# Where the token columns are cut: 384, 352, 352 and 256, 288 in place of 368, 368, 352 and 272, 272

## The chip, the core and the metric

The kernel runs on one core of a Trainium2 chip, as one program. The metric is the device time of one execution in microseconds (us). Before the change the median of three runs is 1601.55 us, the lowest 1600.8 and the highest 1601.77.

## What is computed

One inference step of a two-layer decoder trunk in float32. 1024 tokens of a prompt and 64 tokens of eight samples (eight each) go through the same weights, so there are 1088 token columns. The first layer is a Mamba-2 layer (input projection, short convolution, a chunked scan over the state, a gate, output projection), the second a pooling layer. The parts that matter here are the projections:

```python
def ssd_branch(h, conv_prev, ssm_prev, w_in, ..., w_out):
    zxbcdt = h @ w_in
...
    return gated.astype(h.dtype) @ w_out, new_conv, new_ssm

def pool_branch(h, pool_prev, start_pos, w_in, w_group, ch_scale, w_out):
    uz = h @ w_in
...
    mixed = jnp.einsum('blgc,gcd->blgd', pooled, w_group.astype(jnp.float32)).reshape(b, L, POOL_WIDTH)
    mixed = mixed * ch_scale.astype(jnp.float32) * jax.nn.silu(z)
    return mixed.astype(h.dtype) @ w_out, up[:, -POOL_STATE:]
...
y = rmsnorm(x, final_norm_g).astype(x.dtype)
```

## The kernel before, in words

Activations lie transposed: features on the 128 partitions, the 1088 token columns along the free dimension (64 sample columns last). Every projection is made of TensorE matmuls with a 128x128 weight tile as the stationary operand and a stretch of token columns as the moving one, accumulated in one PSUM tile of up to 512 float32 columns. For precision each operand is split in a high and a low part of type float32r, and each product is three matmuls: high weight by high token, high by low, low by high. Each of the three loads its own weights.

The token columns are cut in two ways.

**Plain projections** (`mm1` and `mm3`, L190 to L192; `op_first`, L807 to L812) cut the 1088 columns by the table `CH` (L21) in three chunks, at 0, 368 and 736, of 368, 368 and 352 columns. A weight tile goes over the three chunks in turn, each in its own PSUM tile. This is how half of the first layer's input projection is done (24 of 48 weight tiles, 20 of them beside the scan), its output projection, the first two tile pairs of the second layer's input projection, and that layer's group products.

**Half products** are used where an algorithm of the Strassen kind replaces eight block products by seven: most of the second layer's input projection and the other half of the first layer's (`fast_pair`, with `product`, L1051 to L1053), and the second layer's output projection (`out_product` with `op_half`, L1269 to L1271). They work on half of the tokens, `HALF` = 544 columns, and cut that half into two quarters of `QUART` = 272 columns, c = 0 and c = 1. In `product` a quarter is four weight tiles by three matmuls, 12 matmuls into one PSUM tile, and then the other quarter with the same weights; in `op_half` it is 8 by 3. `put` and `add` in `fast_pair`, and `contribute` (L1254, L1256), then add the PSUM tiles into sums in SBUF on VectorE, quarter by quarter, and ScalarE copies the first product of each seven out (L1077 and its like).

The end of the program (`pool_layer`, from L1781) runs the last of the seven output products quarter by quarter, so that the final normalization of the quarters that are ready runs beside the last matmuls: a sum of squares over the partitions by a matmul with ones (`ms_log`, L302 and L304), a logarithm and exponentials on ScalarE (L305, L1750, L318), the scaling on VectorE (L1763) and GpSimd (L1761), and the store.

Between the float32r matmuls of the projections stand others in plain float32 (the scan's, transposes, sums of squares). The order on each engine is made by a scheduler from the order of the code and its own estimates of duration.

Of the kernel before, what the change touches and what calls it, by code (L numbers as in the profile page):

```python
# [10 lines left out]
AF = mybir.ActivationFunctionType  # L11
ALU = mybir.AluOpType
# [4 lines left out]
NP = 1024  # L17
NS = 64
TOK = NP + NS
HALF, QUART = TOK // 2, TOK // 4  # L20
CH = ((0, 368), (368, 368), (736, 352))  # L21
KD = 8
EPS = 1e-6
GROUPS = (1, 2, 3, 0)
# [75 lines left out]
class Build:  # L100
# [936 lines left out]
    def product(self, tags, x):  # L1037
        nc = self.nc
        if x not in self.X:
            self.X[x] = [(t[:, :HALF], t[:, HALF:]) for t in (self.T[int(x[1]), k] for k in range(4))]  # L1040
        nxt = next(self.wgen, None)
        if nxt:
            self.wahead.append(nxt)
        else:
            self.stream_split(self.wpos)
        hi, lo = self.wahead.pop(0)
        ps = [self.pp.tile([P, 512], F32, tag=t, bufs={"mm": 3, "tr": 2, "y": 2, "S": 1}[t], name=self.name("st")) for t in tags]
        for c in range(2):
            t = slice(QUART * c, QUART * c + QUART)
            for k, (xh, xl) in enumerate(self.X[x]):  # L1050
                nc.tensor.matmul(ps[c][:, :QUART], hi[:, k], xh[:, t], start=(k == 0), stop=False)  # L1051
                nc.tensor.matmul(ps[c][:, :QUART], hi[:, k], xl[:, t], start=False, stop=False)  # L1052
                nc.tensor.matmul(ps[c][:, :QUART], lo[:, k], xh[:, t], start=False, stop=(k == 3))  # L1053
        return [q[:, :QUART] for q in ps]

    def fast_pair(self, u, z, after):


        nc, product = self.nc, self.product

        def add(out, x, y):
            nc.vector.tensor_tensor(out=out, in0=x, in1=y, op=ALU.add)

        def put(dst, half, c, x, y):
            t, o, rv = dst
            o += HALF * half + QUART * c
            n = QUART - NS if rv is not None and half and c else QUART
            add(t[:, o:o + n], x[:, :n], y[:, :n])
            if n < QUART:
                add(rv, *(v[:, n:].rearrange("p (b i) -> p b i", i=8) for v in (x, y)))  # L1070

        cs = [slice(QUART * c, QUART * c + QUART) for c in range(2)]
# [173 lines left out]
    def contribute(self, m, d, c, ps):  # L1246

        nc, x = self.nc, self.x
        for z, half, sign in SENDS[m]:
            e, a = d + 4 * z, HALF * half + QUART * c  # L1250
            pn = min(a + QUART, NP) - a
            g = (self.gat[1] if sign > 0 else self.ngat)
            g = g[:, e, 8:9] if sign > 0 else g[:, e:e + 1]
            ins = nc.vector.scalar_tensor_tensor(out=x[e][:, a:a + pn], in0=ps[:, :pn], scalar=g, in1=x[e][:, a:a + pn], op0=ALU.mult, op1=ALU.add)  # L1254
            if pn < QUART:
                ins = nc.vector.scalar_tensor_tensor(out=self.sacc[:, e], in0=ps[:, pn:QUART], scalar=float(sign), in1=self.sacc[:, e], op0=ALU.mult, op1=ALU.add)  # L1256
        return ins

    def op_tile(self):
# [3 lines left out]

    def op_half(self, w, blk, ks, c, ps):
        nc, (hi, lo) = self.nc, w
        a = QUART * c
        for k in ks:
            xh, xl = blk[k][:, a:a + QUART], blk[k][:, HALF + a:HALF + a + QUART]
            nc.tensor.matmul(ps[:, :QUART], hi[:, k], xh, start=k == 0, stop=False)  # L1269
            nc.tensor.matmul(ps[:, :QUART], hi[:, k], xl, start=False, stop=False)  # L1270
            nc.tensor.matmul(ps[:, :QUART], lo[:, k], xh, start=False, stop=k == 7)  # L1271

    def out_product(self, m, steps, then=None):

# [397 lines left out]
    def pool_layer(self):  # L1672
        nc, io, sl = self.nc, self.io, self.slots
# [41 lines left out]
        x = self.x = [None] * 8  # L1715
# [18 lines left out]
        for d in range(8):  # L1734
            t = self.mt.tile([P, NS], F32, tag="gs", bufs=2, name=self.name("gs"))
# [37 lines left out]
        blk = self.blocks[7]  # L1773
# [2 lines left out]
            self.ow_fetch()  # L1776
            self.ow_split()
        ws = ws[24:]
        sq, sqs = [], sl.get("sq")
        for c in range(2):  # L1780
            a = QUART * c  # L1781
            for d in range(4):
                ps = self.op_tile()
                self.op_half(ws[d], blk, range(8), c, ps)
                ins = self.contribute(7, d, c, ps)
                if c == 0:
                    with self.tc.issue_after(ins.ins):
# [3 lines left out]
                    square(d, 0, QUART)  # L1791
                else:
                    t = sqs[:, QUART * d:QUART * d + QUART]
                    nc.scalar.activation(t, x[d][:, a:a + QUART], AF.Square)
# [115 lines left out]
```

## Time and profile before

| | before |
|---|---|
| time, median of 3 runs | 1601.55 us |
| span of the profiled execution, first to last instruction | 1599.4 us |
| what lies around the span, by the median | 2.15 us |
| instructions in the trace | 30692 |
| matmul records | 11946 |
| bytes moved by DMA | 275.58 MB |

The profiled execution's own time is known by its span alone. A matmul's row gives its start and its modelled duration; matmuls are pipelined, so that one starts while others are under way. What a matmul costs in a dense stream is therefore the interval from its start to the next one's start, and not the mean duration of its group. A plain float32 matmul has two records in the trace, a float32r matmul has one.

### The profile page before, as it was taken

To read this page: it belongs to the slowest core of one execution; us is meant where nothing else is said; L and a number is where in the kernel's file an instruction comes from. 1 tells how busy PE (TensorE), PEld (TensorE's weight loads), DVE (VectorE), ACT (ScalarE), POOL (GpSimd) and SP (SyncE) were. 2 spreads that over 40 slices of the span, in tenths; PEclk is the share of its full clock that TensorE was granted. 3 is DMA by queue.
4 is the path that set the end of the run, shared out by engine and by line. 5 is a ranking of instruction groups with operands and counts; after the bars stand their busy time and mean duration, and the time that the engine had idled before them with its cause. 6 is when DMAs were issued, how large, how long until landed. Compare 5 with 4: busy or idle time off the path is not lost. (4 is left out here: it accounts for less than half of the span.)

```text
span 1599.4 us, 30692 instructions
## 1 busy us (share of the span) xinstructions
PE 1578.8 (99%) x11946; PEld 1505.4 (94%) x11946; DVE 1293.5 (81%) x2152; ACT 791.4 (49%) x1512; POOL 514.6 (32%) x558
## 2 busy tenths in 40 slices
PE   9999999999999999999999999999999999999997
PEld 7899999998889889888899899999999999999997
DVE  6874879778788888888989867998889867667886
ACT  6663344456676766675455437533323333233364
POOL 0133556512231313131212232275666640000241
PEclk9999999999999999999999999999999999999999
DMA  9423232355555554768899632142333279565683
GB/s 353 166 100 110 69 112 83 110 178 158 188 170 173 161 187 148 240 224 303 289 317 312 221 135 74 60 142 103 114 114 104 102 246 373 142 176 178 165 171 119
DMA packets 122305, 275.58 MB, mean 172 GB/s; under 512 B 18192, under 2 KB 59312, under 8 KB 122160
## 3 DMA queue, kind: packets, MB, share of 16 engines
q1 hardware_dynamic: 118128, 260.90, 47.3%
q0 software_dynamic: 4032, 12.72, 4.7%
q8 instruction: 94, 1.54, 0.4%
q14 instruction: 51, 0.42, 0.1%
HBM read 201.12 MB, written 70.23 MB: 170 GB/s over the span
## 5 line engine op out<-in xcount | busy, mean ns | idle before, releaser
L1051 PE MATMUL st<-hh,w 128*128 128x272 f32 x832 | 240.2, 289 | 0.9 <-ACT w L182 0.9
L1053 PE MATMUL st<-hh,w 128*128 128x272 f32 x832 | 240.4, 289 | 0.4 <-DVE w L184 0.4
L1052 PE MATMUL st<-hl,w 128*128 128x272 f32 x832 | 240.0, 288 | 0.0
L1051 PE MATMUL st<-t,w 128*128 128x272 f32 x624 | 179.7, 288 | 0.0
L1053 PE MATMUL st<-t,w 128*128 128x272 f32 x624 | 179.5, 288 | 0.0
L1052 PE MATMUL st<-t,w 128*128 128x272 f32 x624 | 179.2, 287 | 0.0
L190 PE MATMUL mm<-hh,wh 128*128 128x368 f32 (+1 forms) x528 | 178.3, 338 | 0.0
L192 PE MATMUL mm<-hh,wl 128*128 128x368 f32 (+1 forms) x528 | 173.7, 329 | 0.0
L191 PE MATMUL mm<-hl,wh 128*128 128x368 f32 (+1 forms) x528 | 173.1, 328 | 0.0
L1051 PEld LDWEIGHTS st<-hh,w 128*128 128x128 f32 x832 | 156.8, 188 | 1.4 <-ACT w L182 1.4
L1053 PEld LDWEIGHTS st<-hh,w 128*128 128x128 f32 x832 | 156.5, 188 | 0.9 <-DVE w L184 0.9
L1052 PEld LDWEIGHTS st<-hl,w 128*128 128x128 f32 x832 | 156.7, 188 | 0.0
L182 ACT ACTIVATE w<-wr 128x512 fp32r<-128x512 f32 x104 | 65.1, 631 | 166.2 <-PE st L1053 137.3
L623 POOL TENSOR_TENSOR hd<-h,cd 128x256 f32<-128x256 f32 x56 | 45.9, 820 | 301.0 <-DVE h L624 144.9
L1270 PE MATMUL op<-b,w 128*128 128x272 f32 x448 | 128.9, 288 | 0.8 <-DVE b L1199 0.7
L1269 PE MATMUL op<-b,w 128*128 128x272 f32 x448 | 129.5, 289 | 0.0
L1271 PE MATMUL op<-b,w 128*128 128x272 f32 x448 | 128.9, 288 | 0.0
L190 PE MATMUL mm<-gh,wh 128*128 128x368 f32 (+1 forms) x372 | 125.5, 338 | 0.0
L192 PE MATMUL mm<-gh,wl 128*128 128x368 f32 (+1 forms) x372 | 122.4, 329 | 0.0
L191 PE MATMUL mm<-gl,wh 128*128 128x368 f32 (+1 forms) x372 | 122.0, 328 | 0.2 <-DVE gl L783 0.2
L1051 PEld LDWEIGHTS st<-t,w 128*128 128x128 f32 x624 | 117.7, 189 | 0.1
L1053 PEld LDWEIGHTS st<-t,w 128*128 128x128 f32 x624 | 117.3, 188 | 0.0
(307 smaller groups left out, 4576.5 us busy)
## 6 DMA issues: line engine op xcount, KB each, us to landing
wr<-win SPq DMA_DIRECT2D x48, 512.0 KB, 4.2
acb<-acd SPq DMA_DIRECT2D x64, 256.0 KB, 4.4
wr<-pin SPq DMA_DIRECT2D x32, 512.0 KB, 3.5
wr<-pout SPq DMA_DIRECT2D x28, 512.0 KB, 4.3
x<-x1d SPq DMA_DIRECT2D x24, 544.0 KB, 5.9
x1d<-x SPq DMA_DIRECT2D x22, 544.0 KB, 3.9
wr<-pout POOLq DMA_DIRECT2D x20, 512.0 KB, 6.2
x<-xT SPq DMA_DIRECT2D x16, 544.0 KB, 6.3
```

The source lines that it names most:

```text
L182: self.nc.scalar.activation(hi, src, AF.Copy)
L190: nc.tensor.matmul(ps[:, :n], hi[:, k, :], ah[:, a:a + n], start=first, stop=False)
L191: nc.tensor.matmul(ps[:, :n], hi[:, k, :], al[:, a:a + n], start=False, stop=False)
L192: nc.tensor.matmul(ps[:, :n], lo[:, k, :], ah[:, a:a + n], start=False, stop=last)
L623: nc.gpsimd.tensor_tensor(out=hd, in0=h[-1], in1=cd.unsqueeze(2).to_broadcast([P, 4, 64]), op=ALU.mult)
L1051: nc.tensor.matmul(ps[c][:, :QUART], hi[:, k], xh[:, t], start=(k == 0), stop=False)
L1052: nc.tensor.matmul(ps[c][:, :QUART], hi[:, k], xl[:, t], start=False, stop=False)
L1053: nc.tensor.matmul(ps[c][:, :QUART], lo[:, k], xh[:, t], start=False, stop=(k == 3))
L1269: nc.tensor.matmul(ps[:, :QUART], hi[:, k], xh, start=k == 0, stop=False)
L1270: nc.tensor.matmul(ps[:, :QUART], hi[:, k], xl, start=False, stop=False)
L1271: nc.tensor.matmul(ps[:, :QUART], lo[:, k], xh, start=False, stop=k == 7)
```

## The change

The table `CH` becomes 384, 352, 352 (starts 0, 384, 736). A new table `QCH` holds the two quarters of a half: 256 columns from 0, and 288 columns from 256. Wherever the code said `QUART * c` and `QUART` it now takes the start and the width from `QCH`; the first half's and second half's boundary (544) stays. The number of matmuls, weight loads and evictions stays, and so does the number of columns. Every chunk is then a multiple of 32 columns wide and starts at a multiple of 32 columns from its half's start. At the end of the program the second quarter's squares need 4 x 288 columns, for which the scratch tile is taken from the wider slots (`wide=True`); the final normalization of the first half runs over 256 and 288 columns, that of the second half, which was done before, still over twice 272.

```diff
-CH = ((0, 368), (368, 368), (736, 352))
+CH = ((0, 384), (384, 352), (736, 352))
+QCH = ((0, 256), (256, 288))
...
         for c in range(2):
-            t = slice(QUART * c, QUART * c + QUART)
+            a, n = QCH[c]
+            t = slice(a, a + n)
             for k, (xh, xl) in enumerate(self.X[x]):
-                nc.tensor.matmul(ps[c][:, :QUART], hi[:, k], xh[:, t], start=(k == 0), stop=False)
-                nc.tensor.matmul(ps[c][:, :QUART], hi[:, k], xl[:, t], start=False, stop=False)
-                nc.tensor.matmul(ps[c][:, :QUART], lo[:, k], xh[:, t], start=False, stop=(k == 3))
+                nc.tensor.matmul(ps[c][:, :n], hi[:, k], xh[:, t], start=(k == 0), stop=False)
+                nc.tensor.matmul(ps[c][:, :n], hi[:, k], xl[:, t], start=False, stop=False)
+                nc.tensor.matmul(ps[c][:, :n], lo[:, k], xh[:, t], start=False, stop=(k == 3))
...
-            o += HALF * half + QUART * c
-            n = QUART - NS if rv is not None and half and c else QUART
+            o += HALF * half + QCH[c][0]
+            w = QCH[c][1]
+            n = w - NS if rv is not None and half and c else w
...
-            e, a = d + 4 * z, HALF * half + QUART * c
-            pn = min(a + QUART, NP) - a
+            e, a, n = d + 4 * z, HALF * half + QCH[c][0], QCH[c][1]
+            pn = min(a + n, NP) - a
...
-        a = QUART * c
+        a, n = QCH[c]
         for k in ks:
-            xh, xl = blk[k][:, a:a + QUART], blk[k][:, HALF + a:HALF + a + QUART]
+            xh, xl = blk[k][:, a:a + n], blk[k][:, HALF + a:HALF + a + n]
...
-        sq, sqs = [], sl.get("sq")
-        for c in range(2):
-            a = QUART * c
+        sq, sqs = [], sl.get("sq", wide=True)
+        for c, (a, n) in enumerate(QCH):
...
-                            p = norm(0, QUART)
-                            scale(0, QUART, p, ((4, 5, 6, 7), (0, 1, 2, 3)), (0, 4))
-        p1 = norm(QUART, QUART, sq)
-        scale(QUART, QUART, p1, ((4, 5), (6, 7), (0, 1), (2, 3)), (4, 6))
+                            p = norm(*QCH[0])
+                            scale(*QCH[0], p, ((4, 5, 6, 7), (0, 1, 2, 3)), (0, 4))
+        p1 = norm(*QCH[1], sq)
+        scale(*QCH[1], p1, ((4, 5), (6, 7), (0, 1), (2, 3)), (4, 6))
```

How the instructions stand, on two places of TensorE. The first is the passage from the first quarter to the second in a half product of the second layer's input projection (`st` is the PSUM tile, `t` a token block, `w` a weight block), before:

```order
L1051 MATMUL st_13562<-t_12137,w_13463 128x272
L1052 MATMUL st_13562<-t_12137,w_13463 128x272
L1053 MATMUL st_13562<-t_12137,w_13463 128x272
L1051 MATMUL st_13563<-t_11988,w_13463 128x272
L1052 MATMUL st_13563<-t_11988,w_13463 128x272
L1053 MATMUL st_13563<-t_11988,w_13463 128x272
```

and after:

```order
L1053 MATMUL st_13562<-t_12137,w_13463 128x256
L1054 MATMUL st_13562<-t_12137,w_13463 128x256
L1055 MATMUL st_13562<-t_12137,w_13463 128x256
L1053 MATMUL st_13563<-t_11988,w_13463 128x288
L1054 MATMUL st_13563<-t_11988,w_13463 128x288
L1055 MATMUL st_13563<-t_11988,w_13463 128x288
```

Nothing has moved there; only the widths differ. The second place is beside the scan of the first layer, where the scheduler threads the scan's matmuls (`S` the chunk's state, `y` its rows) into a plain projection (`mm`), before:

```order
L192 MATMUL mm_4294<-hh_407,wl_4023 128x352
L190 MATMUL mm_4294<-hh_469,wh_4022 128x352
L615 MATMUL S_4244<-xd_4211,Bt_4213 128x256
L637 MATMUL y_4278<-M_4202,xd_4211 64x128 x2
L637 MATMUL y_4279<-M_4202,xd_4211 64x128 x2
L191 MATMUL mm_4294<-hl_470,wh_4022 128x352
```

and after:

```order
L193 MATMUL mm_4294<-hh_407,wl_4023 128x352
L616 MATMUL S_4244<-xd_4211,Bt_4213 128x256
L191 MATMUL mm_4294<-hh_469,wh_4022 128x352
L638 MATMUL y_4278<-M_4202,xd_4211 64x128 x2
L638 MATMUL y_4279<-M_4202,xd_4211 64x128 x2
L192 MATMUL mm_4294<-hl_470,wh_4022 128x352
```

The state's matmul stands one matmul earlier than before; there are some dozens of such shifts by one to three places along the program, on TensorE and, to match, on the engines that work with it.

More of the change, by code (lines that the diff above doesn't have):

```diff
@@ L1065, in put @@
             t, o, rv = dst
-            o += HALF * half + QUART * c
-            n = QUART - NS if rv is not None and half and c else QUART
+            o += HALF * half + QCH[c][0]
+            w = QCH[c][1]
+            n = w - NS if rv is not None and half and c else w
             add(t[:, o:o + n], x[:, :n], y[:, :n])
-            if n < QUART:
+            if n < w:
                 add(rv, *(v[:, n:].rearrange("p (b i) -> p b i", i=8) for v in (x, y)))
-        cs = [slice(QUART * c, QUART * c + QUART) for c in range(2)]
+        cs = [slice(a, a + n) for a, n in QCH]
         s = self.tp.tile([P, HALF], F32, tag="mt2", bufs=self.nmt2, name=self.name("u2"))
@@ L1254, in contribute @@
             ins = nc.vector.scalar_tensor_tensor(out=x[e][:, a:a + pn], in0=ps[:, :pn], scalar=g, in1=x[e][:, a:a + pn], op0=ALU.mult, op1=ALU.add)
-            if pn < QUART:
-                ins = nc.vector.scalar_tensor_tensor(out=self.sacc[:, e], in0=ps[:, pn:QUART], scalar=float(sign), in1=self.sacc[:, e], op0=ALU.mult, op1=ALU.add)
+            if pn < n:
+                ins = nc.vector.scalar_tensor_tensor(out=self.sacc[:, e], in0=ps[:, pn:n], scalar=float(sign), in1=self.sacc[:, e], op0=ALU.mult, op1=ALU.add)
         return ins
@@ L1265, in op_half @@
         nc, (hi, lo) = self.nc, w
-        a = QUART * c
+        a, n = QCH[c]
         for k in ks:
-            xh, xl = blk[k][:, a:a + QUART], blk[k][:, HALF + a:HALF + a + QUART]
-            nc.tensor.matmul(ps[:, :QUART], hi[:, k], xh, start=k == 0, stop=False)
-            nc.tensor.matmul(ps[:, :QUART], hi[:, k], xl, start=False, stop=False)
-            nc.tensor.matmul(ps[:, :QUART], lo[:, k], xh, start=False, stop=k == 7)
+            xh, xl = blk[k][:, a:a + n], blk[k][:, HALF + a:HALF + a + n]
+            nc.tensor.matmul(ps[:, :n], hi[:, k], xh, start=k == 0, stop=False)
+            nc.tensor.matmul(ps[:, :n], hi[:, k], xl, start=False, stop=False)
+            nc.tensor.matmul(ps[:, :n], lo[:, k], xh, start=False, stop=k == 7)
     def out_product(self, m, steps, then=None):
@@ L1790, in pool_layer @@
                             square(5 + d, 0, HALF)
-                    square(d, 0, QUART)
+                    square(d, 0, n)
                 else:
-                    t = sqs[:, QUART * d:QUART * d + QUART]
-                    nc.scalar.activation(t, x[d][:, a:a + QUART], AF.Square)
+                    t = sqs[:, n * d:n * d + n]
+                    nc.scalar.activation(t, x[d][:, a:a + n], AF.Square)
                     sq.append(t)
```

2 lines of the change are left out of this document (1 added, 1 removed).

## The prediction

> **What bounds the kernel now.** I read the head of the profile's page first, then what TensorE waited for, then its groups, and last single stretches of it in order of time.
>
> ```profile
> span 1599.4 us, 30692 instructions
> PE 1578.8 (99%) x11946; PEld 1505.4 (94%) x11946; DVE 1293.5 (81%) x2152; ACT 791.4 (49%) x1512; POOL 514.6 (32%) x558
> PEclk9999999999999999999999999999999999999999
> ```
>
> TensorE is busy in 99% of the span, at full granted clock throughout. VectorE, the next, stands at 81%. A busy TensorE could still be one that is held up, so the waits come next:
>
> ```profile
> PE mm L807 <- ACT raw L434: 1.7, 1, 1.7
> PE y L637 <- DVE M L587: 1.3, 1, 1.3
> PE warm L245 <- DVE ones L217: 1.1, 1, 1.1
> ...
> PE pl L191 <- DVE x L339: 0.2, 1, 0.2
> ```
>
> The longest wait in the whole program is 1.7 us, the seventeen listed come to some 13 us, and each happens once or twice. So the end is set by how fast TensorE gets through its list. What a matmul of that list costs is the interval to the next start, which the mean duration of a group doesn't give. How many there are of each width, by the groups with their shapes kept apart and by the count of two lines over the whole span:
>
> ```profile
> L1051 PE MATMUL st<-hh,w 128*128 128x272 f32 x832 | 240.2, 289 | 0.9 <-ACT w L182 0.9
> L1051 PE MATMUL st<-t,w 128*128 128x272 f32 x624 | 179.7, 288 | 0.0
> L1269 PE MATMUL op<-b,w 128*128 128x272 f32 x448 | 129.5, 289 | 0.0
> L190 PE MATMUL mm<-hh,wh 128*128 128x368 f32 x352 | 120.2, 341 | 0.0
> L190 PE MATMUL mm<-hh,wh 128*128 128x352 f32 x176 | 58.1, 330 | 0.0
> ...
> 0.00:1600.00 1600.00, 412.70 (x1236) 231.56 (x1236) 1.00 0.52 172
> ...
> 0.00:1600.00 1600.00, 4.22 (x12) 2.25 (x12) 1.00 0.52 172
> ```
>
> The half products have 832 + 624 + 448 = 1904 matmuls on the first of their three lines, so 3 x 1904 = 5712 of 272 columns. The plain projections have 1236 on L190 and 12 on L807, 1248 in all, and as many on the other two lines: 3744, two of 368 columns to one of 352 (352 to 176 in the pair of rows), that is 1248 triples of 368, 368 and 352.
>
> Now the intervals. A stretch of 210 us in the second layer's input projection holds nothing on TensorE but half products:
>
> ```profile
> 1040.00:1250.00 210.00, 210.00 (x1676) 210.00 (x1676) 185.97 (x264) 63.27 (x110) 138.25 (x104) 1.00 0.32 113
> ```
>
> 210 us over 1676 matmuls is 125.3 ns for 272 columns. For the plain widths, three rows of the timeline in the group products: the first matmul of two 368 tiles, the first of the 352 tile that follows, the first of the tile after that.
>
> ```profile
> 1340.45 0.33 PE L190 MATMUL mm<-ph,wh 128*128 128x368 f32 x1
> ...
> 1344.48 0.32 PE L190 MATMUL mm<-ph,wh 128*128 128x352 f32 x1
> ...
> 1346.38 0.33 PE L190 MATMUL mm<-ph,wh 128*128 128x368 f32 x1
> ```
>
> 24 matmuls of 368 in 4.03 us are 167.9 ns each, 12 of 352 in 1.90 us are 158.3 ns each. With these prices the three kinds fill 5712 x 125.3 + 2496 x 167.9 + 1248 x 158.3 ns = 715.7 + 419.1 + 197.6 = 1332 us of the 1599.
>
> **The question the change turns on.** It keeps the number of matmuls and of columns, so it can only win if an interval isn't one straight line in the width. From 272 to 352 columns the interval grows by 33.0 ns, 0.41 ns a column; from 352 to 368 by 9.6 ns, 0.60 ns a column. On the line through 272 and 352, 368 columns would take 164.9 ns: they lose 3.0 ns. 352 is 11 times 32; 368 and 272 are not multiples of 32. The line through the two that aren't has a slope of (167.9 - 125.3) / 96 = 0.44 ns a column and would put 352 at 160.8; it does 2.5 ns better. So the trace shows a kink that fits the rule of 32, but three widths don't say whether 272 carries the loss too, or 368 alone. One more reading helps, the two quarters of one half product (the block B22), its first row, the first row of its second quarter, and the first row of what follows:
>
> ```profile
> 1102.91 0.29 PE L1051 MATMUL st<-hh,w 128*128 128x272 f32 x1
> ...
> 1104.42 0.29 PE L1051 MATMUL st<-hh,w 128*128 128x272 f32 x1
> ...
> 1105.91 0.29 PE L1051 MATMUL st<-t,w 128*128 128x272 f32 x1
> ```
>
> 12 matmuls in 1.51 us are 125.8 ns each, the next 12 of the same width in 1.49 us are 124.2. So a part of a loss is in the 272s, and it hangs on where the columns start as well as on how many there are.
>
> **The change, part by part.** Terms are made against the profiled span and put on the median; the 2.15 us between the two stay as they are.
>
> Plain projections. A triple costs 2 x 167.9 + 158.3 = 494.1 ns now. Afterwards it is 384, 352 and 352. The trace has no 384. On the line through 272 and 352 it would take 171.5, on a line of slope 0.44 through 352 it would take 172.5, and if it carried on from 368 with that one's loss, 167.9 + 16 x 0.41 = 174.5. The second 352 starts at column 384 instead of 736; it costs 158.3 at best and 160.8 if it lies like a width that loses. The triple is then 488.1 at best and 174.5 + 160.8 + 158.3 = 493.6 at worst. I take 172.5 and twice 158.3, 489.1, because 352 is the nearest row that shares the property that 384 has. That is 5.0 ns a triple, and 1248 x 5.0 ns = 6.2 us gained (ends 7.5 and 0.6).
>
> Half products. The pair is 2 x 125.3 ns now. On the line through 272 and 352, 256 columns take 118.7 and 288 take 131.9, mean 125.3: nothing gained. On the line of slope 0.44 through 352 they take 115.7 and 129.9, mean 122.8: 2.5 ns gained on each of 5712, 14.3 us. I take a quarter of it, 0.6 ns and 3.4 us, because the two quarters above, 1.6 ns apart, show that some places already run without most of the loss and that the place matters, which the change only sets in part. Ends 0 and 14.3.
>
> The evictions work on as many columns as before, in pieces of 256 and 288 or 384 and 352, and as many pieces. The cover is TensorE's own list: in the stretch of half products VectorE is busy 185.97 us of 210. If TensorE got 2.5 ns faster on each of the 1676, the stretch would be 4 us shorter and VectorE at 90%, still not the later of the two. If that cover were gone, VectorE would be what the next step is late for, but by these rows that isn't reached. The matmuls of the scan, which stand a place earlier or later, cost what they did; a wait that comes of it is bounded by the longest of that kind above, 1.3 us (`y` behind `M`), and TensorE's whole list is queued behind it, so I count it in the range and not in the sum. The wider scratch tile at the end is written and read by the same instructions; I count nothing for it.
>
> The end of the program gets longer, since its last quarter has 288 columns and not 272. Its rows, in order of time after the last product:
>
> ```profile
> 1588.98 2.00 PE L304 MATMUL ms<-sq,ones 128*128 128x272 f32 x8
> ...
> 1591.01 0.49 ACT L305 ACTIVATE rst<-ms,eps 128x272 f32<-128x272 f32 x1 [0.91 <-PE ms L304]
> 1591.53 0.40 ACT L1750 ACTIVATE ms<-rst 128x272 f32<-128x272 f32 x1
> ...
> 1591.97 2.54 DVE L1763 SCALAR_TENSOR_TENSOR y<-x,vec,ms 128x272 f32<-128x272 f32 x6 [2.33 <-ACT ms L1750]
> ```
>
> They come to 5.4 us in line with one another, and 16/272 of that is 0.3; with the store's 6% more bytes behind them I take 0.4 us lost.
>
> Sum: 1601.55 - 6.2 - 3.4 + 0.4 = 1592.35, so I say 1592.3. With the ends of both terms the same mechanism gives 1601.55 - 7.5 - 14.3 + 0.4 = 1580.1 and 1601.55 - 0.6 + 0.4 = 1601.4; most of its weight lies between 1585 and 1598.
>
> **The rivals.**
>
> *The columns alone count.* The interval may just bend upwards: if each column past 352 costs the 0.60 ns that the step to 368 shows, 384 takes 167.9 + 16 x 0.60 = 177.5, and 177.5 + 158.3 is 335.8, exactly two 368s. With the halves on the line of 0.41, nothing is gained but the tail's 0.4 lost: 1601.9. For it: 272 and 352 lie on one line with no loss in 272. Against it: the 1.6 ns between two quarters of one width. [...] Chance 0.21.
>
> *All of the loss goes.* The 272s carry the full 2.5 ns, and both tables of widths lose it: 1601.55 - 14.3 - 6.2 + 0.4 = 1581.5. For it: the kink is read off the same three intervals. Against it: the quarter that does better by itself, which then has less to gain. Chance 0.10.
>
> *Slower: the short quarter can't use its fewer columns.* Every matmul loads its own weights, and if something beside the columns, the load above all, holds the interval near 125 ns, 272 already lies on that floor, 256 stays at 125.3, and 288 pays its columns, 131.9. The mean is 128.6, 3.3 ns more on 5712, 18.8 us: 1601.55 + 18.8 - 6.2 + 0.4 = 1614.6. The point from which it decides: the plain gain less the tail, 5.8 us, is 1.0 ns on each of 5712, so it is slower as soon as 256 takes over 120.7 ns with 288 at 131.9. For it: no float32r matmul in the trace is as narrow as 256. Against it: the warm-up at the start runs float32 matmuls with as many weight loads as matmuls,
>
> ```profile
> 6.00:14.00 8.00, 8.00 (x74) 8.00 (x73) 5.33 (x5) 5.59 (x6) 0.00 (x0) 1.00 1.01 406
> ```
>
> 73 loads of 128 columns in 8.00 us, one in 110 ns, under the 118.7 that 256 columns should take; but those are plain float32, and the room is only 9 ns. Chance 0.10.
>
> **How the numbers follow.** The forecast's case, a part of the loss recovered, gets 0.59, the three rivals 0.21, 0.10 and 0.10. A measurement of this kernel can tell about 0.2%, 3.2 us, from no change. Faster is the forecast's case and the full recovery, 0.69; the same is the columns alone, 0.21; slower is the floor, 0.10. The time is that of the likeliest, 1592.3. The range has to reach the columns alone at 1601.9, so up to 1602.5, and goes down to 1584, a little below where most of the forecast's own weight ends; it leaves out the full recovery and the floor, 2 in 10.
>
> **What would show it.** In the same stretch of half products the matmuls alternate 12 of 256 and 12 of 288; the step is right if the mean interval is about 124.7 ns, 256 near 118 and 288 near 131. Columns alone: 125.3 again. Full recovery: 122.8. The floor: 256 above 120.7. In the group products a 384 should take about 172.5 ns and both 352s about 158; 177.5 would be the bend, and 160.8 at the 352 that starts at column 384 would say that the place and not the width loses. The end, from the last product's last matmul to the last instruction, should be some 0.4 us longer. The list of waits should stay as short as it is; a wait of TensorE on VectorE at L1065 and below, repeated at every product, would make the forecast wrong in a way that none of the rivals has.

## The result, and the profile after

The changed kernel takes 1612.37 us (median of 4 runs, 1612.16 to 1612.95) against 1601.66 us for the kernel before (4 runs, 1600.8 to 1605.08): a ratio of 1.0061 [1.0047, 1.0075], slower by some 10 us where 9 us of gain were forecast. The profiled execution took 1612.22 us and its span is 1610.4, 11.0 more than before. Lines of the changed kernel have numbers one to three higher than those of before, so its L1055 is before's L1053.

The head of the page first. The last row shown is TensorE in 40 slices of the span:

```profile
span 1610.4 us, 30703 instructions
...
PE 1582.2 (98%) x11946; PEld 1508.2 (94%) x11946; DVE 1294.5 (80%) x2152; ACT 790.1 (49%) x1512; POOL 524.1 (33%) x558
...
PE   9999999999999999999999999899999999999997
```

The busy time of every engine but GpSimd is almost what it was (TensorE 1578.8 before); GpSimd's grew from 514.6 to 524.1 us. But one digit, the 26th, is an 8: the slice from 1006.5 to 1046.8 us, in which TensorE stood for a while. The waits of TensorE name it (line waited for: us in total, times, longest):

```profile
PE st L1055 <- DVE w L185: 6.1, 4, 4.2
PE S L616 <- ACT Bt L594: 2.3, 4, 0.7
PE mm L808 <- ACT raw L435: 1.6, 1, 1.6
```

The first row is new; before had no wait over 1.7 us. Half products wait for a split weight, in one place. The windows (PE, PEld, DVE, ACT, POOL, then the granted clock, the DMA share and GB/s) frame it, before:

```profile
1030.00:1040.00 10.00, 10.00 (x82) 10.00 (x81) 9.26 (x17) 4.92 (x11) 3.79 (x3) 1.00 0.38 127
1040.00:1050.00 10.00, 10.00 (x82) 10.00 (x82) 7.18 (x16) 3.64 (x6) 5.39 (x7) 1.00 0.46 161
1050.00:1250.00 200.00, 200.00 (x1596) 200.00 (x1596) 178.79 (x249) 59.63 (x104) 132.86 (x98) 1.00 0.32 110
```

and after:

```profile
1030.00:1040.00 10.00, 5.75 (x37) 5.55 (x36) 4.87 (x7) 3.85 (x7) 0.00 (x0) 0.78 0.31 107
1040.00:1050.00 10.00, 8.56 (x59) 8.35 (x59) 9.96 (x17) 5.53 (x12) 2.23 (x2) 0.88 0.31 108
1050.00:1250.00 200.00, 200.00 (x1596) 200.00 (x1595) 177.41 (x259) 60.63 (x105) 128.99 (x98) 1.00 0.35 116
```

In the 20 us from 1030 on TensorE began 96 matmuls instead of 164. The 68 that are missing are 68 x 125.3 ns = 8.5 us. In the 200 us behind that it began 1596, as before: the new halves run no faster there and no slower. So most of the loss is one stop at the opening of the second layer's half products. The two traces laid side by side, matmul by matmul, say the same: the changed kernel is 1.8 us late when the first half product of the second layer starts, 10.4 us late when the stop is over, and 11.0 at the end.

**The widths themselves.** The same reading of the timeline as in the prediction, first rows of tiles, now in the changed kernel: a 288 quarter, the 256 and 288 quarters of the next product, and the quarter behind them; then a 384 tile, its two 352s and the next 384:

```profile
1105.75 0.30 PE L1053 MATMUL st<-hh,w 128*128 128x288 f32 x1
...
1107.33 0.28 PE L1053 MATMUL st<-t,w 128*128 128x256 f32 x1
...
1108.74 0.30 PE L1053 MATMUL st<-t,w 128*128 128x288 f32 x1
...
1110.33 0.28 PE L1053 MATMUL st<-t,w 128*128 128x256 f32 x1
...
1351.08 0.34 PE L191 MATMUL mm<-ph,wh 128*128 128x384 f32 x1
...
1353.19 0.32 PE L191 MATMUL mm<-ph,wh 128*128 128x352 f32 x1
...
1355.12 0.32 PE L191 MATMUL mm<-ph,wh 128*128 128x352 f32 x1
...
1357.03 0.34 PE L191 MATMUL mm<-ph,wh 128*128 128x384 f32 x1
```

12 matmuls of 256 take 1.41 us, 117.5 ns each; 12 of 288 take 1.59, 132.5 each. 12 of 384 take 2.11 us, 175.8 ns, and the two 352s 160.8 and 159.2. Single readings are good to about 1 ns. The mean over the matmuls whose successor works on the same tile, without the intervals that a wait or another matmul in between makes longer by a quarter or more, gives, in ns: 256 118.4, 272 125.25, 288 132.8, 352 158.9 before and 159.9 after, 368 167.8, 384 174.5. Inside the quarters the pair of halves goes from 2 x 125.25 to 251.2. With the step from one quarter to the next, in which a 256 takes 117.5 ns and a 288 132.1, it comes to 251.06, +0.27 ns on each of 5712, +1.5 us. Nearly all of that is in the first layer, where the mean of all intervals between half products goes from 125.3 to 125.8 ns; in the second layer, from 1050 to 1250 us, it goes from 125.45 to 125.50. The triple goes from 494.59 to 494.33, -0.3 us on 1248. The tail is the same: from the row of eight sums of squares at the end to the span's end, 10.4 us in both. With the stop's 8.5 that makes 9.7 of the 11.0 us; the other 1.3 lies in small waits that I can't assign.

**What the stop is made of.** The order of the engines at the opening, before: GpSimd's first sum of the weights, the VectorE instruction beside it, SyncE's store of the first gate tile, and ScalarE's split that needs the buffer which that store frees:

```profile
1009.88 1.80 POOL L1016 TENSOR_TENSOR sw<-wr 128x512 f32<-128x512 f32 x1 [8.78 <-PE pl L191]
1010.45 2.31 DVE L145 TENSOR_TENSOR wl<-wr,wh 128x1024 fp32r<-128x1024 f32 x1
...
1018.24 0.37 SPq L925 DMA_DIRECT2D zgd<-pz  x1
...
1024.08 0.66 ACT L978 ACTIVATE t<-x 128x544 fp32r<-128x544 f32 x1 [3.00 <-DMA zgd<-pz]
```

and the same after, with the links between them and the matmuls that waited:

```profile
1012.64 12.16 POOL L1017 TENSOR_TENSOR sw<-wr 128x512 f32<-128x512 f32 x1 [7.83 <-PE pl L192]
1013.49 1.22 DVE L146 TENSOR_TENSOR wl<-wr,wh 128x1024 fp32r<-128x1024 f32 x1
...
1022.92 0.72 DVE L976 TENSOR_TENSOR x<-x,x 128x544 f32<-128x544 f32 x1
1024.87 1.28 POOL L1018 TENSOR_TENSOR sw<-sw,wr 128x512 f32<-128x512 f32 x1
...
1027.46 0.29 POOL L900 COPY npl<-u 128x120 f32<-128x120 f32 x1
1027.78 0.34 SPq L901 DMA_DIRECT2D npT<-npl  x1
...
1028.69 0.38 SPq L926 DMA_DIRECT2D zgd<-pz  x1
1034.44 0.66 ACT L979 ACTIVATE t<-x 128x544 fp32r<-128x544 f32 x1 [11.94 <-DMA zgd<-pz]
1035.13 0.72 DVE L980 TENSOR_TENSOR t<-x,t 128x544 fp32r<-128x544 f32 x1 [11.49 <-ACT t L979]
1036.40 0.69 DVE L185 TENSOR_TENSOR w<-wr,w 128x512 fp32r<-128x512 f32 x1
1037.14 0.58 PE L1055 MATMUL st<-hh,w 128*128 128x256 f32 x1 [4.25 <-DVE w L185]
1037.52 0.41 PE L1053 MATMUL st<-hh,w 128*128 128x256 f32 x1
...
1039.44 0.44 PE L1053 MATMUL st<-hh,w 128*128 128x288 f32 x1
...
1042.32 0.29 PE L1053 MATMUL st<-t,w 128*128 128x256 f32 x1
```

Read from the top: the same addition of 512 columns takes 12.16 us instead of 1.80; the next one, with VectorE quiet, takes 1.28. Through all of that time VectorE goes from one two-input instruction to the next, each at its normal length (the split of the stream's weights 1.22 us; before it was stretched to 2.31, and the two engines took turns). GpSimd ends 1.2 us after VectorE's run has ended. In GpSimd's queue stand the two small copies of the pool's last rows; in SyncE's queue their store (`npT`), and behind it a load of weights and the gate tile's store; behind that store's data ScalarE's split, behind ScalarE VectorE, behind VectorE the weight that TensorE needs. TensorE waits 6.1 us in four pieces, and from 1037.52 to 1039.44 nine matmuls of 256 take 213 ns each instead of 118: the clock had fallen (0.50 granted from 1035.50 to 1042.33 us, which makes the 0.78 and 0.88 of the two windows above). The 21 matmuls from 1037.52 to 1042.32, nine of 256 and twelve of 288, lose 9 x 95 + 12 x 107 ns = 2.1 us by that. Waits and slow matmuls are 8.2 of the 8.5 us.

What the trace shows of the blocking is these lengths, 12.16 us beside VectorE's run against 1.28 with VectorE quiet; by what means the one engine keeps the other out was not shown. Of the clock it shows when: TensorE's last matmul in front of the wait of 4.25 us ends at 1032.90, the granted clock goes from 1.00 to 0.50 at 1035.50, 2.6 us later, and is 1.00 again from 1042.33 on. A stretch that is idle only in part was enough elsewhere: in e12, described below, no wait at the opening is over 1.9 us, TensorE was busy 7.21 of the 10 us from 1030 to 1040, and the granted clock was 0.84 in the mean of these 10 us.

### The profile page after: what moved, and what is told of

It is laid out like the page before. It is cut to its first block, busy times and chain, and to the rows that moved or that the text cites. A ratio compares the mean times of both kernels' runs of the same rounds, so it can differ in the third digit from the quotient of the medians.

```text
span 1610.4 us, 30703 instructions
## 1 busy us (share of the span) xinstructions
PE 1582.2 (98%) x11946; PEld 1508.2 (94%) x11946; DVE 1294.5 (80%) x2152; ACT 790.1 (49%) x1512; POOL 524.1 (33%) x558
## 4 chain that ended last, share of the span: by engine, by line
PE 79%; DVE 7%; DMA 5%; issue 4%; ACT 4%; POOL 1%; SPq 0%; DVEq 0%; ACTq 0%; POOLq 0%
PE st L1055 10%; PE mm L191 10%; PE st L1054 10%; PE st L1053 10%; PE mm L192 9%; PE mm L193 9%; PE op L1273 2%; PE op L1274 2%; PE op L1272 2%; DMA acb<-acd 2%; PE y L638 2%; PE S L616 2%; PE y L642 1%; PE am L262 1%; PE tr L577 1%
## 5 line engine op out<-in xcount | busy, mean ns | idle before, releaser
L1055 PE MATMUL st<-hh,w 128*128 128x256 f32 (+1 forms) x832 | 241.8, 291 | 4.7 <-DVE w L185 4.7
L1053 PE MATMUL st<-hh,w 128*128 128x256 f32 (+1 forms) x832 | 241.6, 290 | 0.7 <-ACT w L183 0.7
L1054 PE MATMUL st<-hl,w 128*128 128x256 f32 (+1 forms) x832 | 241.1, 290 | 0.0
L1055 PE MATMUL st<-t,w 128*128 128x256 f32 (+1 forms) x624 | 179.7, 288 | 1.4 <-DVE w L185 1.4
L1054 PE MATMUL st<-t,w 128*128 128x256 f32 (+1 forms) x624 | 179.7, 288 | 0.0
L191 PE MATMUL mm<-hh,wh 128*128 128x352 f32 (+1 forms) x528 | 179.2, 339 | 0.1
L1053 PE MATMUL st<-t,w 128*128 128x256 f32 (+1 forms) x624 | 179.2, 287 | 0.0
L193 PE MATMUL mm<-hh,wl 128*128 128x352 f32 (+1 forms) x528 | 172.7, 327 | 0.0
L192 PE MATMUL mm<-hl,wh 128*128 128x352 f32 (+1 forms) x528 | 172.6, 327 | 0.0
L1055 PEld LDWEIGHTS st<-hh,w 128*128 128x128 f32 x832 | 158.1, 190 | 5.3 <-DVE w L185 5.3
L1053 PEld LDWEIGHTS st<-hh,w 128*128 128x128 f32 x832 | 158.1, 190 | 1.1 <-ACT w L183 1.1
L1273 PE MATMUL op<-b,w 128*128 128x256 f32 (+1 forms) x448 | 129.2, 288 | 0.9 <-DVE b L1202 0.9
L1272 PE MATMUL op<-b,w 128*128 128x256 f32 (+1 forms) x448 | 129.5, 289 | 0.0
L1274 PE MATMUL op<-b,w 128*128 128x256 f32 (+1 forms) x448 | 128.6, 287 | 0.0
L191 PE MATMUL mm<-gh,wh 128*128 128x384 f32 (+1 forms) x372 | 125.6, 338 | 0.1
L192 PE MATMUL mm<-gl,wh 128*128 128x384 f32 (+1 forms) x372 | 122.1, 328 | 0.1
L193 PE MATMUL mm<-gh,wl 128*128 128x384 f32 (+1 forms) x372 | 121.7, 327 | 0.0
L1055 PEld LDWEIGHTS st<-t,w 128*128 128x128 f32 x624 | 117.5, 188 | 1.6 <-DVE w L185 1.6
L1053 PEld LDWEIGHTS st<-t,w 128*128 128x128 f32 x624 | 117.4, 188 | 0.2 <-issue 0.2
```

What stands on the lines that cost most here:

```text
L191: nc.tensor.matmul(ps[:, :n], hi[:, k, :], ah[:, a:a + n], start=first, stop=False)
L192: nc.tensor.matmul(ps[:, :n], hi[:, k, :], al[:, a:a + n], start=False, stop=False)
L193: nc.tensor.matmul(ps[:, :n], lo[:, k, :], ah[:, a:a + n], start=False, stop=last)
L1053: nc.tensor.matmul(ps[c][:, :n], hi[:, k], xh[:, t], start=(k == 0), stop=False)
L1054: nc.tensor.matmul(ps[c][:, :n], hi[:, k], xl[:, t], start=False, stop=False)
L1055: nc.tensor.matmul(ps[c][:, :n], lo[:, k], xh[:, t], start=False, stop=(k == 3))
```

## The experiments

Theory A: the widths are neutral to 2 us and the loss is the one stop, by the chain above. Theory B: the new widths themselves cost the time, spread over the program. Each kernel was compared with the kernel before on the same chip (medians of before 1601.58 to 1602.24 us); "sum" is the first GpSimd instruction at the opening that can be held out, "wait" TensorE's longest there.

| kernel | ratio to before | sum, us | wait, us |
|---|---|---|---|
| after | 1.0061 [1.0047, 1.0075] | 12.16 | 4.2 |
| e1 new halves only | 1.0014 [1.0006, 1.0023] | 1.79 | none |
| e2 new plain chunks only | 1.0063 [1.0051, 1.0075] | 12.15 | 4.1 |
| e3 after, small stores off SyncE | 1.0020 [1.0011, 1.0028] | 20.43 | none |
| e4 after, sums on VectorE | 1.0047 [1.0034, 1.0060] | 9.99 (a copy) | 2.4 |
| e5 odd widths | 1606.18 us, one run | 12.15 | 3.5 |
| e6 after, old chunks at the opening | 1.0073 [1.0053, 1.0093] | 11.58 | 4.2 |
| e7 before, small stores off SyncE | 0.9998 [0.9990, 1.0007] | 1.80 | none |
| e8 plain chunks only, small stores off SyncE | 1.0012 [1.0003, 1.0021] | 20.44 | none |
| e9 after, splits in another order | 1.0120 [1.0104, 1.0136] | 12.75 | 5.8 |
| e10 before, sum asked for later | 1.0000 [0.9992, 1.0009] | 1.78 | none |
| e11 after, sum asked for later | 1.0062 [1.0048, 1.0075] | 10.17 (a copy) | 1.9 |
| e12 after, VectorE waits for the sum | 1.0035 [1.0023, 1.0048] | 6.38 | 1.9 |

**The two tables of widths apart.** e1 has the new halves alone, e2 the new plain chunks alone:

```
e1: CH = ((0, 368), (368, 368), (736, 352));  QCH = ((0, 256), (256, 288))
e2: CH = ((0, 384), (384, 352), (736, 352));  QCH = ((0, 272), (272, 272))
```

> Plain chunks back to 368, 368, 352; quarters 256 and 288 as changed. Theory A (widths neutral, one stall): the pair 256 + 288 costs 251.2 ns against 250.5 for twice 272, so 5712 x 0.35 ns = 2.0 us, and the stall at the opening of the second layer is gone because the plain pairs there run as before: 1601.7 + 2.0 + 0.3 at the end = 1604 us, TensorE's waits as short as before. Theory B (the widths themselves cost it, the halves above all): 1610 to 1612 us.

> Plain chunks 384, 352, 352 as changed; quarters back to 272 twice. Theory A: the triple costs 494.3 ns against 494.6, nothing; the stall of about 8.5 us at the opening of the second layer comes with the plain chunks and stays: 1610 us, with a GpSimd addition of over 10 us at L1017 and VectorE idle behind it. Theory B, with the cost in the quarters: 1601 to 1602 us.

1605.1 us and 1612.16. The whole loss comes with the plain chunks, the term that was to bring most of the gain, though their matmuls start at the same intervals as in the changed kernel (384 174.5 ns, 352 159.8). e1's +2.2 us (1.0 to 3.7 by its ratio) is of the size of the 1.5 of its intervals; that the intervals are all of it isn't shown, for its profiled execution, the slowest of eleven, lost more than that in small waits. GpSimd's sum in e1,

```profile
1013.47 1.79 POOL L1017 TENSOR_TENSOR sw<-wr 128x512 f32<-128x512 f32 x1 [8.77 <-PE pl L192]
```

and in e2, and under it the window of e2's stop:

```profile
1009.63 12.15 POOL L1017 TENSOR_TENSOR sw<-wr 128x512 f32<-128x512 f32 x1 [8.22 <-PE pl L192]
```

```profile
1030.00:1040.00 10.00, 5.07 (x24) 4.63 (x24) 8.00 (x12) 6.97 (x15) 0.00 (x0) 0.83 0.07 25
```

**The link in SyncE's queue.** e3 is the changed kernel with the small store that waits for GpSimd moved to GpSimd's own queue, for the first two tiles:

```
-        nc.sync.dma_start(self.io["npT"][p], npl)
+        (nc.gpsimd if p < PLAIN else nc.sync).dma_start(self.io["npT"][p], npl)
```

> The changed kernel, with the store of the pool state of the first two tiles issued from GpSimd's queue instead of SyncE's. Theory A: SyncE's queue no longer stands behind the late GpSimd copies, the store that frees the slot goes out when its data is ready, ScalarE and VectorE do not stop, and TensorE's stall goes: 1612.4 - 8.5 = 1604 us, though the GpSimd addition may still take over 10 us. Theory B: 1612 us, unchanged.

1605.34 us. GpSimd is held out even longer, but the gate tile's store no longer stands behind that, and the stop is gone (first the timeline, then the window):

```profile
1012.56 20.43 POOL L1017 TENSOR_TENSOR sw<-wr 128x512 f32<-128x512 f32 x1 [7.85 <-PE pl L192]
...
1018.62 17.10 SPq L926 DMA_DIRECT2D zgd<-pz  x2
```

```profile
1030.00:1040.00 10.00, 9.63 (x77) 9.43 (x76) 6.63 (x9) 4.49 (x9) 8.41 (x7) 1.00 0.19 67
```

So the late sum alone costs little: TensorE began 156 matmuls from 1030 to 1050 us where before began 164, 8 x 125 ns = 1.0 us. What costs is what SyncE has queued behind it. e7 does the same to the kernel before, e8 to the kernel with the new plain chunks alone:

> The kernel before with the two small stores of the first pool tiles on GpSimd's queue in place of SyncE's, nothing else. A control for the run that did the same to the changed kernel and took some 7 us off it. Theory A (that gain was the stop going): here, where there is no stop, no change, 1601 to 1602.5. Theory B (those stores cost SyncE's queue time whatever the widths): 1594 to 1597.

> The new plain chunks 384, 352, 352 with the old halves of 272 twice, and the two small stores of the first pool tiles off SyncE's queue. What is left of the change's loss is now the plain chunks alone, without the stop. Theory A (the plain widths are neutral, the halves of 256 and 288 cost the 2 to 3 us that the runs without the stop still lose): 1601 to 1603, at most 0.1 per cent from the kernel before. Theory B (the plain chunks cost something besides the stop): 1604 to 1606, as with the new halves.

1601.72 us: the edit by itself is worth nothing. And 1604.09: without the stop the plain chunks lose 1.9 us (0.5 to 3.4), not the 10.1 of e2. The median lies in B's range; A had at most 0.1%, which the interval reaches as well. About 1 us of it is visible: behind the sum of 20.44 us TensorE began 74 matmuls from 1030 to 1040 where before began 82. The rest I can't place.

**Any GpSimd instruction there is held out.** e4 puts the first three sums on VectorE:

```
+            eng = nc.vector if n == 16 - PLAIN and i == 0 else nc.gpsimd
-            nc.gpsimd.tensor_tensor(out=s[:, f], in0=z[:, f], in1=z[:, l], op=ALU.add)
+            eng.tensor_tensor(out=s[:, f], in0=z[:, f], in1=z[:, l], op=ALU.add)
```

(and the same for the two behind it)

> The changed kernel, with the first three weight sums of the second layer on VectorE instead of GpSimd. Theory A: no GpSimd operation stands beside the dense VectorE work there, the copies behind it come early, SyncE's queue moves on, and the stall goes: 1604 us, up to 1 us more for three additions of about 0.7 us on a VectorE that is late there. Theory B: 1612 us or more.

1609.93 us: a miss for both. The stop got shorter, not away, because the next in GpSimd's queue, a copy of 15 columns, now stood in front of the same run:

```profile
1014.48 9.99 POOL L899 COPY npl<-u 128x15 f32<-128x15 f32 x1 [8.72 <-ACT u L890]
```

**Is 32 anything?** e5 takes widths off the multiples; it was run once, for its profile:

```
CH = ((0, 400), (400, 336), (736, 352))
QCH = ((0, 264), (264, 280))
```

> The changed kernel with its six widths moved off the multiples of 32: plain chunks of 400, 336 and 352, halves of the half products in 264 and 280. Only the time from one matmul's start to the next inside a tile is read, and whether TensorE stops at the opening of the second layer. Theory A (a matmul costs its columns plus a rest that only creeps up with width; nothing turns on 32): 264 and 280 lie on the line between their neighbours, about 122 and 129 ns, together 250.5 to 251.5; 400 about 181.5, 336 about 152.5, the three plain chunks together 493.5 to 495.5. Theory B (a width that is a multiple of 32 is cheaper than its neighbours, so that the changed kernel's widths are the good ones and something else makes them dear): 264 and 280 together over 253.5, the plain chunks together over 497. On the time neither says much: A 1602 to 1613, by whether the stop returns.

264 takes 121.7 ns and 280 takes 128.95, together 250.7; 400, 336 and 352 take 180.8, 153.3 and 159.9, together 494.0. As A had it, and 0.5 and 0.3 ns less than the multiples of 32 take: nothing turns on 32. The stop came back here too. Until it began, this one trace was 3.4 us ahead of before's, and the intervals explain little of that; with a single execution it stays an observation.

**Where does the condition come from?** e6 gives the old chunks back to the opening's plain tiles alone (`OPEN` holds 368, 368, 352):

```
-        for c, ch in enumerate(CH):
+        for c, ch in enumerate(OPEN):
```

> The changed kernel with the old chunks of 368, 368 and 352 in one place alone, the twelve plain tiles of the first two tiles of pool and gate at the opening of the second layer; every other plain projection keeps 384, 352, 352 and the halves keep 256 and 288. Theory A (widths are neutral; one stop of about 8.5 us, set by which engine's instructions meet VectorE's run at that opening): the pool tiles' copies out come back to the old spacing, GpSimd's first sum of the weights takes about 1.8 us again instead of 12.2, SyncE's store of the gate tile goes out near 1018 us instead of 1028, TensorE has no wait over 1.5 us there, and the kernel takes 1603.5 to 1605.5. Theory B (the new widths themselves cost the 10 us, spread over the layers): 1611 to 1613, since 12 tiles of some hundreds are changed back. Theory C (what decides is the state in which the first layer leaves the engines, not the opening itself): the sum takes 12 us all the same, 1611 to 1613, with the stop in its place.

1615.09 us, the sum at 11.58: a miss for A. The sum is what C said, the time lies above its range. What decides is not the opening's own widths; it comes in from the first layer, or from the order that the scheduler makes. One of its six runs took 1604.96, the others 1612.49 to 1616.84, so it may turn from one execution to the next; only one was profiled.

e9 was meant to put breaks into VectorE's run, with the split that needs the newest result first:

```
+            new(4, k, r[:, h1])
             new(2, k, r[:, h2])
             new(3, k, p[:, h2])
             yield
-            new(4, k, r[:, h1])
```

> The changed kernel with one thing in another order at the opening of the second layer: of the three splits that follow each step's four subtractions on VectorE, the one that needs the newest result comes first, so that VectorE has to wait some tenths of a microsecond for ScalarE's copy, four times in all. No instruction is added or left out. Theory A (GpSimd's first sum of the weights is held out because VectorE's instructions follow one another with no break, and gets in at the first break): the sum takes under 6 us instead of 12.2, SyncE's store of the gate tile goes out 6 us earlier or more, TensorE has no wait over 2.5 us there, and the kernel takes 1604 to 1607. Theory B (breaks of that length do not let GpSimd in, or it is another thing that holds it out): the sum takes 10 us or more, the stop stays, 1611 to 1615.

1620.15 us, outside both. VectorE's rows show no break from 1008.46 to 1023.03: ScalarE's copies were there in time, so the condition that was to be tested did not come about. The stop got longer (5.8 us on ScalarE's split, then 2.7 on VectorE's), and another 4.6 us were lost between 1540 and 1580 us, which says only that this order is worse.

e10 and e11 fill the sum's tile with zeros first, so that the sum is asked for about 1 us later, e10 in the kernel before, e11 in the changed one:

```
+            if n == 16 - PLAIN and i == 0:
+                nc.gpsimd.memset(s, 0.0)
```

> The kernel before, all its widths as they were, with one instruction more on GpSimd: it fills the tile of the first sum of the weights with zeros before the sum is formed, which makes GpSimd ask for that sum later, by the time of the fill, and leaves the values as they are. Theory A (the changed kernel's stop depends on where in VectorE's run GpSimd's request falls, and on nothing that the widths do to TensorE): if the request falls into VectorE's unbroken run, the sum or the fill takes 10 us or more, TensorE stops as it does in the changed kernel, and the kernel takes 1609 to 1614 with its old widths; if it still finds a break, 1601 to 1603. Theory B (the stop belongs to the new widths): 1601 to 1603, with the sum at 1.3 to 2.5 us, wherever the request falls.

> The changed kernel with the same fill ahead of the first sum of the weights that the kernel before was given in the run named e10_before_late_sums: GpSimd writes zeros into the sum's tile, a write that VectorE's rows did not stretch there, and asks for the sum's own reads about 1 us later. Theory A1 (GpSimd is let in when its request falls early in a VectorE instruction, and held out when it falls late in one: 0.07 to 0.08 us against 0.36 to 0.44 us into it in the traces so far): the later request falls about 0.1 us into the 1.22 us split of the stream's weights, is let in at its end, the sum takes under 4 us, no stop, 1604 to 1606. Theory A2 (GpSimd is let in only by a break in VectorE's run, and there is none here): the sum, or the copies behind it, takes 9 us or more, the stop stays, 1610 to 1614. Theory B (the new widths): 1611 to 1613, whatever the sum takes.

1602.32 us and 1611.66. In e10 GpSimd got in and the engines took turns, which both theories allow, so it doesn't tell them apart:

```profile
1011.58 0.96 POOL L1017 MEMSET sw<- 128x1024 f32 x1 [8.76 <-PE pl L191]
...
1013.41 1.78 POOL L1018 TENSOR_TENSOR sw<-wr 128x512 f32<-128x512 f32 x1
...
1013.95 1.82 DVE L979 TENSOR_TENSOR t<-x,t 128x544 fp32r<-128x544 f32 x1
```

In e11 the fill passed as freely, and then a copy of 15 columns that asked 0.04 us into VectorE's split was held out for the rest of the run:

```profile
1015.65 0.96 POOL L1018 MEMSET sw<- 128x1024 f32 x1 [7.81 <-PE pl L192]
1016.56 10.17 POOL L899 COPY npl<-u 128x15 f32<-128x15 f32 x1
```

So it isn't the moment within an instruction (A1 falls; the copy asked early and was held out), and it is GpSimd's instructions that read that are held out, not one that only writes. The stop and 1611.66 us are what A2 said; by the time alone B said the same.

e12 makes VectorE wait for the sum, with a copy of 4 columns in VectorE's queue behind it:

```
             nc.gpsimd.tensor_tensor(out=s[:, f], in0=z[:, f], in1=z[:, l], op=ALU.add)
+            if n == 16 - PLAIN and i == 0:
+                nc.vector.tensor_copy(s[:, 4:5, 0:4], s[:, 0:1, 0:4])
```

> The changed kernel with one instruction more on VectorE: a copy of 4 columns of the first sum of the weights onto columns of the same tile that are written over afterwards, so that no value changes. It stands in VectorE's queue five instructions behind the split of the stream's weights, and VectorE must wait there until GpSimd's sum is done. Theory A (VectorE's unbroken run keeps GpSimd out, that makes SyncE's store late, and the late store makes the stop): the sum, asked for near 1012.6 us, ends when VectorE comes to its wait, after 5.5 to 7 us instead of 12.2, the store of the gate tile goes out 4 us earlier or more, TensorE has no wait over 2.5 us at the opening, 1604 to 1607; the wait of VectorE itself, 1 to 2 us, is hidden. Theory B (VectorE is the late engine there, and any wait added to it makes the stop longer): 1613 to 1616.

1606.86 us: with one instruction and one wait added, 5.5 us less than the changed kernel by the medians, 4.2 by the two ratios:

```profile
1010.81 6.38 POOL L1017 TENSOR_TENSOR sw<-wr 128x512 f32<-128x512 f32 x1 [8.22 <-PE pl L192]
...
1017.23 0.17 DVE L1019 COPY sw<-sw 128x4 f32<-128x4 f32 x1 [1.19 <-POOL sw L1017]
1017.30 2.55 DVE L906 TENSOR_TENSOR ws<-u 128x1222 f32<-128x1222 f32 x1
...
1021.57 13.83 SPq L926 DMA_DIRECT2D zgd<-pz  x2
```

GpSimd's sum ends 1.2 us after VectorE begins to wait, after 6.38 us instead of 12.16, from there on the two take turns (2.55 us for a row that takes 1.43 alone), and the store goes out 10.8 us after the sum was asked for instead of 16.1. Theory A for the chain holds; B falls.

**What stays open.** Why VectorE's run is open to GpSimd in before, e1, e7 and e10 and shut in the ten others. Two things go with it in all fourteen traces. The order of VectorE's queue in front of the split of the stream's weights is one and the same in the four, and another in the ten. Before (the split itself, at 1010.45, is shown above):

```profile
1008.53 0.72 DVE L975 TENSOR_TENSOR x<-x 128x544 f32<-128x544 f32 x1
1009.17 1.36 DVE L975 TENSOR_TENSOR x<-x,x 128x544 f32<-128x544 f32 x2
```

and after (the split at 1013.49):

```profile
1011.58 1.36 DVE L976 TENSOR_TENSOR x<-x 128x544 f32<-128x544 f32 x2
1012.85 0.72 DVE L976 TENSOR_TENSOR x<-x,x 128x544 f32<-128x544 f32 x1
```

And VectorE's semaphore wait in front of that split lasts 0.22 us in the four, 0.05 in the ten. That wait is no break in VectorE's work, whose rows on both sides of it start 0.63 to 0.64 us apart in before and after alike, and it ends 0.36 us before GpSimd asks in before, 0.24 in after. So a new order of the queue, which the scheduler makes when the widths change, is as good a candidate as a shift in time. e6's one execution of 1604.96, with the order unchanged, would speak for time, but it wasn't profiled; no run changed the one without the other. Which of the first layer's plain projections moves it wasn't tried. No version beat the kernel before: every pair and triple of widths measured lies within 0.7 ns of the old one.

## Why the prediction was wrong

**Plain projections, -6.2 us: measured -0.3.** The step that failed in its working is "the nearest row that shares the property that 384 has": the kink between 352 and 368 was read as a loss of widths off 32. What the intervals show is a rest above columns / 2.4 (2.4 columns a ns are an estimate, twice the 1.2 measured at a granted clock of 0.50, 256 columns in 213 ns). It grows, not evenly, from 11.7 ns at 256 to 14.5 at 368 and 384 and falls again to 14.1 at 400. At the 352s it is between 12.2 and 13.9, by the kernel and the place. 384 takes 174.5, the value that the prediction had for "carried on from 368 with that one's loss", its worst case. The 352 at column 384 takes 160.5 against 159.4 at 736 (means in one kernel), so the place, or what runs in front of it, is worth 1 ns, within the ends given.

**Half products, -3.4 us: measured +1.5.** 256 was put at about 118 and is 118.4, 288 at about 131 and is 132.8. The term's own lower end, nothing gained, was still too hopeful; the two quarters of unequal speed before told of the place, as the text said, but not of a loss that a new width would recover.

**Evictions and cover, nothing: measured 8.5 us.** This is the step that made the sign wrong: "by these rows that isn't reached", and a new wait "bounded by the longest of that kind above, 1.3 us". VectorE's share in the stretch of half products was the right check for that stretch, and there it held (177.4 us of 200). It was not made for the 20 us before it, from 1020 to 1040, where VectorE was already busy 9.81 and 9.26 of 10 us and feeds the first half products, and where GpSimd and SyncE stand in between. The bound was taken from a wait behind one instruction; this one, 6.1 us in four pieces, goes through five queues, and 2.1 us of half clock come with it. (The seventeen waits of the list add up to 11.7 us and not to "some 13"; nothing hangs on that.) The last sentence named a wait of TensorE on VectorE as what would make the forecast wrong outside all rivals. It came, at L1055, but once and not at every product.

**The tail, +0.4: measured 0.0.** Too small to matter.

**The rivals.** *The columns alone count* was nearest on the widths: e3, which has both tables and not the stop, took 1605.34, 3.4 us above its 1601.9; its 177.5 for a 384 was too much. *All of the loss goes* had nothing to recover. *Slower: the floor* came near the time by chance, 1614.6, and is refuted as a cause: 256 is at 118.4, under its deciding point of 120.7. The slowing was none of the rivals.

## What to carry to other kernels

Before a change of tile widths is priced by intervals, look for the places where a queue feeds TensorE just in time: a small change of order or time there can be worth more than all the intervals together, as it was here (8.5 us against 1.2). A store that waits for GpSimd is better kept out of a queue in which something urgent stands behind it: e3 won back some 7 us by moving two such stores, and e7 lost nothing by it. A kink seen in three widths is no rule about widths; a run with more widths off the supposed grid, as e5's 264, 280 and 400, settles it for the range measured.

## What the runs showed of the hardware that was not expected

- A run of back-to-back two-input VectorE instructions kept a GpSimd instruction that reads SBUF out from its first request to the end of the run: 12.16 us for 1.28 us of work, 20.44 in e8, 9.99 and 10.17 for a copy of 15 columns that takes 0.20 alone. A pure write passed beside it in 0.96 us and stretched nothing.
- Where GpSimd got in (before, e1, e7 and e10, and e12 behind a wait of VectorE), the two took turns instruction by instruction, with the same instructions: mostly 1.76 to 1.82 us for additions that take 0.72 us on VectorE or 1.28 on GpSimd alone.
- After a stop of 4.25 us TensorE ran at half clock (0.50 granted) until 1042.33, 213 ns for 256 columns and 240 for 288. That is columns / 1.2 with no rest: the 11.7 to 14.5 ns above columns / 2.4 are not there at half clock.
- A stop of that length isn't needed: in e12 and e11 no wait at the opening is over 1.9 us, and the granted clock was 0.84 in e12 from 1030 to 1040 us, with TensorE busy 7.21 of the 10, and 0.66 in e11 from 1040 to 1050, with 6.52 busy.
